# All big products of a hybrid attention block as seven block products instead of eight

## The chip, the core and the metric

The kernel runs on one core of a Trainium2 chip. Its time is the device time of one execution in microseconds, and the median of three runs is given. The engines work side by side, each with its own queue in order: TensorE (PE, with its loads of the stationary operand as PEld), VectorE (DVE), ScalarE (ACT), GpSimd (POOL), and SyncE (SP), whose queue issues nearly all transfers. A queue whose first instruction waits holds everything behind it.

## The reference

One layer over 512 tokens of width 2048 in float32:

```python
h = rms_norm(x, norm_gain)                       # 512 x 2048
proj = einsum('bsd,de->bse', h, w_in)            # 2048 -> 7184 columns
(sb_q, sb_k, sb_v, sb_g, gl_q, gl_k, gl_v, gl_g, gl_lr) = split(proj)
# group A: 8 heads x 128, q and k normed per head, stick-breaking attention
a_out = rms_norm(stick_breaking(q, k, v), sb_o_gain) * silu(sb_g)
# group B: 4 heads, gated linear attention; the decay comes from the 16 columns gl_lr
b_out = rms_norm(gla(gl_q, gl_k, gl_v, log_alpha), gla_o_gain) * silu(gl_g)
x = x + einsum('bse,ed->bsd', concat(a_out, b_out), w_out)   # 2048 -> 2048
```

The two einsums are the big products: 14 column groups of 512 in w_in (the 16 columns gl_lr apart) and 4 in w_out, each 512 tokens x 2048 x 512.

## The kernel before, in words

Every float32 operand of a big product is split into hi + lo, both of a format that TensorE takes in one pass (hi rounded by ScalarE, lo = value - hi by VectorE), and a product is the sum of three terms hi·hi, hi·lo, lo·hi. The 16 contraction tiles of h stay in SBUF as h_hi and h_lo for the whole kernel (lines 202 to 211); x is scaled by the norm's gain alone, and 1/rms of each token (rstd, rbc) is put in after the products.

`product` (line 173) makes one column group: four PSUM banks (128 tokens, or 128 columns, each), eight units of two contraction tiles. A unit's weights come from `weight_unit` (line 158): one 512 KB load by SP into a tile "st" (a ring of three), one cast on ScalarE, one subtraction on VectorE (tiles "hi" and "lo", rings of three), then 24 matmuls of 512 columns. Loads, splits and copies out of PSUM are under `urgent()`, which puts them ahead of other work of their engine.

Between the chunks of the products TensorE does the small work: the norm of x (`x_norm`, line 258: loads of x, squares on ScalarE, rstd, then four small matmuls that spread rstd along the free axis, bank rbc_ps), the gate ranks (`ranks`, `decays`), the attention heads and the GLA heads. These are chains of Python generators (class `Sides`): each step yields an amount of TensorE's work that shall lie before its next step, or a condition. TensorE's order is just the order in which the program is written out, so a step that finds its operands late stops TensorE; the other engines' orders are set by a scheduler when the kernel is built.

The order of the products (from line 632): q, k, v of the first four heads, the same of the other four, v, k, q and v of GLA, four groups of gates, four groups of the output. GpSimd makes constants and the masks of the attention (`affine_select`, lines 536 and 543).

Of the kernel before, what the change touches and what calls it, by code (L numbers as in the profile page):

```python
# [7 lines left out]
F32 = mybir.dt.float32  # L8
# [11 lines left out]
NU = NK // KU  # L20
NG_IN = 14           # 512-column groups of w_in (the 16 gate-rank columns apart)
# [10 lines left out]
NWK, NWT, NRING = 7, 6, 25      # tiles of the rings  # L32
URGENT = 1500                  # priority of what the tensor engine waits for
LAT_W = 14.0                   # tensor engine's work to put between a bank of scores and its weights
LAT_O = 12.0                   # the same, between an output and its normed value


class Sides:
# [42 lines left out]
def body(ctx: ExitStack, tc: tile.TileContext, x, xT, w_in, w_lr, w_alpha, vecs, w_out, out):  # L81
# [3 lines left out]
    hpool = ctx.enter_context(tc.tile_pool(name="hpool", bufs=1))  # L85
# [3 lines left out]
    ring = ctx.enter_context(tc.tile_pool(name="ring", bufs=1))  # L89
    pacc = ctx.enter_context(tc.tile_pool(name="pacc", bufs=4, space=PSUM))  # L90
# [32 lines left out]
    def room(n):  # L123
        return lambda: held[0] + n <= NRING

    def spl(name):
        return work.tile([P, S], F32R, name=name, tag="spl", bufs=8)
# [9 lines left out]
    def evac(dst, src, scale=None):  # L137
        """Copies that free a bank, by the two engines in turn."""
# [19 lines left out]
    def weight_unit(src, tag, beside=None):  # L158
        with urgent():
            st = wpool.tile([P, KU, S], F32, name=f"st_{tag}", tag="st", bufs=3)  # L160
# [12 lines left out]
    def product(src, a_hi, a_lo, tmajor, tag, before=None):
        """Four banks of a 512-column group; a_* hold the contraction on partitions."""
        acc = [pacc.tile([P, S], F32, name=f"acc_{tag}_{j}", tag="acc") for j in range(4)]
        for u in range(NU):
            beside = before(u) if before is not None else None
            hi, lo = weight_unit(src[u], f"{tag}_{u}", beside)
            for j in range(4):
                for i in range(KU):  # L180
                    k = u * KU + i
                    js = slice(j * P, (j + 1) * P)
                    first, last = k == 0, k == NK - 1
                    if tmajor:
                        terms = [(a_hi[k][:, js], hi[:, i, :]), (a_hi[k][:, js], lo[:, i, :]),
                                 (a_lo[k][:, js], hi[:, i, :])]
# [556 lines left out]
```

## Time and profile before

| | |
|---|---|
| median of 3 runs | 892.63 us (891.7 to 892.99) |
| span of the profiled execution, first to last instruction | 889.4 us |
| TensorE busy | 879.2 us, 99% |
| VectorE, ScalarE, GpSimd busy | 412.4, 364.7, 38.4 us |
| moved by DMA | 93.17 MB, mean 105 GB/s |

The span is the time inside the profiled execution; the timed runs also hold what lies around it. Busy is the time in which an engine had an instruction under way. Matmuls overlap, so their own durations (0.39 us) are longer than the distance from one start to the next; the distance is what counts. The granted clock of TensorE is 1.00 in every stretch.

### The profile page before, as it was taken

How to read it: one execution, taken by the hardware profiler on the slowest of the kernel's cores; microseconds unless marked ns; L12 is line 12 of the kernel's file. 1: busy time of each engine (PE TensorE's matmuls, PEld its weight loads, DVE VectorE, ACT ScalarE, POOL GpSimd, SP SyncE). 2: the span in 40 equal slices, each digit the busy share in tenths (PEclk: the TensorE clock that was granted, in tenths of full speed). 3: DMA queues.
4: the chain of work that ended last, by engine and by line, in shares of the span. 5: the costliest groups of instructions: out<-in, count | busy, mean ns of one | idle time of the engine just before them, and what ended most of it. 6: DMA issues, size and time to landing. Idle time of an engine off the chain costs nothing.

```text
span 889.4 us, 10463 instructions
## 1 busy us (share of the span) xinstructions
PE 879.2 (99%) x4090; PEld 728.9 (82%) x4090; DVE 412.4 (46%) x578; ACT 364.7 (41%) x712; POOL 38.4 (4%) x84
## 2 busy tenths in 40 slices
PE   8999999999999999999999999999999999999998
PEld 6888888888888887788888888888888888888886
DVE  6352343667545378655333444372727363232321
ACT  6762522467463276554112433372626362111110
POOL 1000000111000011210000000000000000000000
PEclk9999999999999999999999999999999999999999
DMA  9841222222222222122222221223232244443521
GB/s 340 283 142 50 95 94 95 71 80 87 72 71 94 76 72 72 67 71 86 95 102 73 71 77 66 74 93 99 100 104 100 95 143 147 137 165 120 177 83 48
DMA packets 30497, 93.17 MB, mean 105 GB/s; under 512 B 3536, under 2 KB 3664, under 8 KB 30448
## 3 DMA queue, kind: packets, MB, share of 16 engines
q1 hardware_dynamic: 28000, 88.29, 29.2%
q10 hardware_dynamic: 2448, 4.21, 1.3%
q8 instruction: 32, 0.52, 0.2%
q14 instruction: 17, 0.14, 0.0%
HBM read 88.30 MB, written 4.19 MB: 104 GB/s over the span
## 4 chain that ended last, share of the span: by engine, by line
PE 86%; issue 7%; DVE 3%; ACT 1%; POOL 1%; DMA 0%; SPq 0%; POOLq 0%; DVEq 0%; ACTq 0%
PE acc_g L99 20%; PE acc_o L99 20%; PE acc_k L99 10%; PE acc_q L99 10%; PE acc_sv L99 6%; PE acc_gv L99 5%; PE acc_gq L99 5%; PE acc_gk L99 4%; PE a L99 2%; PE o L99 1%; PE lr_ps L99 1%; PE kv L99 1%; DMA st_q<-in_w_in 0%; PE zB L99 0%; DVE cs_A L539 0%
## 5 line engine op out<-in xcount | busy, mean ns | idle before, releaser
L99 PE MATMUL acc_g<-h_hi,hi_g 128*128 128x512 f32 x256 | 101.4, 396 | 0.0
L99 PE MATMUL acc_g<-h_hi,lo_g 128*128 128x512 f32 x256 | 99.7, 390 | 0.0
L99 PE MATMUL acc_g<-h_lo,hi_g 128*128 128x512 f32 x256 | 99.6, 389 | 0.0
L99 PE MATMUL acc_o<-hi_o,mh 128*128 128x512 f32 x256 | 99.6, 389 | 0.0
L99 PE MATMUL acc_o<-lo_o,mh 128*128 128x512 f32 x256 | 99.6, 389 | 0.0
L99 PE MATMUL acc_o<-hi_o,ml 128*128 128x512 f32 x256 | 99.6, 389 | 0.0
L170 DVE TENSOR_TENSOR lo_o<-st_o,hi_o 128x1024 fp32r<-128x1024 f32 x32 | 39.2, 1224 | 110.1 <-ACT hi_o L169 101.7
L169 ACT CAST hi_o<-st_o 128x1024 fp32r<-128x1024 f32 x32 | 33.7, 1053 | 125.6 <-PE acc_o L99 116.8
L170 DVE TENSOR_TENSOR lo_g<-st_g,hi_g 128x1024 fp32r<-128x1024 f32 x32 | 39.2, 1223 | 74.4 <-ACT hi_g L169 74.4
L169 ACT CAST hi_g<-st_g 128x1024 fp32r<-128x1024 f32 x32 | 33.6, 1049 | 72.6 <-PE acc_g L99 65.9
L99 PEld LDWEIGHTS acc_g<-h_hi,lo_g 128*128 128x128 f32 x256 | 48.0, 188 | 10.2
L99 PEld LDWEIGHTS acc_o<-lo_o,mh 128*128 128x128 f32 x256 | 48.0, 188 | 10.1
L99 PEld LDWEIGHTS acc_o<-hi_o,mh 128*128 128x128 f32 x256 | 48.0, 188 | 10.0
L99 PEld LDWEIGHTS acc_g<-h_lo,hi_g 128*128 128x128 f32 x256 | 48.1, 188 | 9.8
L99 PEld LDWEIGHTS acc_o<-hi_o,ml 128*128 128x128 f32 x256 | 48.0, 188 | 9.8
L99 PEld LDWEIGHTS acc_g<-h_hi,hi_g 128*128 128x128 f32 x256 | 48.1, 188 | 9.6
L99 PE MATMUL acc_gv<-hi_gv,h_hi 128*128 128x512 f32 x128 | 52.1, 407 | 0.0
L99 PE MATMUL acc_k<-hi_k,h_hi 128*128 128x512 f32 x128 | 51.9, 405 | 0.0
L99 PE MATMUL acc_q<-hi_q,h_hi 128*128 128x512 f32 x128 | 50.5, 395 | 1.1 <-ACT hi_q L169 1.1
L99 PE MATMUL acc_sv<-hi_sv,h_hi 128*128 128x512 f32 x128 | 51.0, 398 | 0.0
L99 PE MATMUL acc_q<-lo_q,h_hi 128*128 128x512 f32 x128 | 50.0, 391 | 0.2 <-DVE lo_q L170 0.2
L99 PE MATMUL acc_k<-hi_k,h_lo 128*128 128x512 f32 x128 | 50.2, 392 | 0.0
(275 smaller groups left out, 1754.5 us busy)
## 6 DMA issues: line engine op xcount, KB each, us to landing
st_g<-in_w_in SPq DMA_DIRECT2D x32, 512.0 KB, 3.2
st_o<-in_w_out SPq DMA_DIRECT2D x32, 512.0 KB, 3.3
st_k<-in_w_in SPq DMA_DIRECT2D x16, 512.0 KB, 3.3
st_sv<-in_w_in SPq DMA_DIRECT2D x16, 512.0 KB, 3.2
st_gv<-in_w_in SPq DMA_DIRECT2D x16, 512.0 KB, 3.2
st_q<-in_w_in SPq DMA_DIRECT2D x15, 512.0 KB, 3.3
xk<-in_xT SPq DMA_DIRECT2D x16, 256.0 KB, 5.9
xt<-in_x SPq DMA_DIRECT2D x16, 256.0 KB, 5.2
```

What stands on the lines that cost most here:

```text
L99: nc.tensor.matmul(o, l, r, **kw)
L169: nc.scalar.copy(hi[:, p, :], st[:, p, :])
L170: nc.vector.tensor_tensor(lo[:, p, :], st[:, p, :], hi[:, p, :].bitcast(F32), ALU.subtract)
```

## The change

The tokens are cut in two halves of 256, the contraction in two halves (even and odd tiles), and the columns in two groups of 512. The eight products of such blocks become seven, with sums of blocks as operands (Strassen's scheme). `pair` does two column groups in four stages; in each stage it goes through four units of two contraction tiles (256 tokens x 256 of the contraction on the left, 256 of the contraction x 512 columns on the right):

- stage one: A11·B11 into the banks x, D·(B11 + B12) into y;
- stage two: NQ·(pw + B22) into x, S4·B22 into y;
- stage three: A12·B21 into y, S3·(pw - B11) into x; in the last unit these two are turned round;
- stage four: A22·(pw + B21) into x.

Here pw is a tile per unit ("pw", a ring of four) that holds the running sum of weight blocks. B11, B22, B21 and B11 once more are loaded into "st" (still a ring of three); in the order their names end in a, b, c and d and the unit's number. The sums of weights are made by VectorE but the last, pw + B21, by GpSimd. The sums of blocks of h (D, NQ, S4, S3) are made in the first pair by GpSimd and split there; D and S3 stay in SBUF, the other five split operands are written to DRAM ("far") and loaded again in every later pair, 512 KB per unit, into a ring of three tiles ("as"). Partial results leave the banks between the stages (stash) and are added at the end (finish). The pairs are (q0, k0), (q1, v0), (v1, k1), (GLA q, GLA k), (GLA v), two pairs of gates and two of the output. The third pair has the ranks' small matmuls between its block products, on its own left operands. In the pair "gqk" the weights are the stationary side and the 256 tokens the moving one, so its matmuls have 256 columns; in the others they keep 512. The output's left operand gets the same seven sums in its first pair. The gates and norms are rewritten for tiles of two halves, with the same arithmetic but for one activation less in the SiLU.

```diff
+    def load(src, tag, part="st"):
+            t = wpool.tile([P, KU, S], F32, name=f"{part}_{tag}", tag=part, bufs=HU if part == "pw" else 3)
+            nc.sync.dma_start(t, src)
+        return t
+
+    def split(t, tag):
+        with urgent():
+            nc.scalar.copy(hi, t)
+            nc.vector.tensor_tensor(lo, t, hi.bitcast(F32), ALU.subtract)
+    def add(o, a, b, op=ALU.add, eng=None):
+        with urgent():
+            (eng or nc.vector).tensor_tensor(o, a, b, op)
...
+                    t = work.tile([P, 2, KU, H2], F32R, name=name, tag="as", bufs=NAS)
+                    if key in self.far:
+                        nc.sync.dma_start(t.bitcast(F32), self.far[key])
+                        return t
...
+                if f not in self.keep:
+                    far = dram.tile([P, 2, KU, H2], F32, name=f"far_{name}")
+                    self.far[key] = far
+                    nc.sync.dma_start(far, t.bitcast(F32))
...
+        def mult(f, u, w, acc, start, stop):
+            t = A.get(f, u)
+            hi, lo = w
+            if tmajor:
+                for a in range(2):
+                    js = slice(a * P, (a + 1) * P)
+                    for i in range(KU):
+                        ah, al = t[:, 0, i, js], t[:, 1, i, js]
+                        for n, (l, r) in enumerate(((ah, hi[:, i]), (ah, lo[:, i]), (al, hi[:, i]))):
+                            mm(acc[a], l, r, start=start and i == 0 and n == 0,
+                               stop=stop and i == KU - 1 and n == 2, skip_group_check=True)
...
+        for u in order:
+            if before is not None:
+                before(0, u)
+            b11, pw[u] = load(s1[u], f"{tag}a{u}"), load(s2[u], f"{tag}{u}", "pw")
+            w = split(b11, f"{tag}a{u}")
+            mult("A11", u, w, x, u == first, u == last)
+            if before is not None:
+                before(1, u)
+            add(pw[u], pw[u], b11)
+            w = split(pw[u], f"{tag}p{u}")
+            mult("D", u, w, y, u == first, u == last)
+        m1 = o1.stash(x, 0, 1.0, f"{tag}m1")
+        m5 = o2.stash(y, 1, -1.0, f"{tag}m5")
+        for u in order:
+            if before is not None:
+                before(2, u)
+            b22 = load(s2[HU + u], f"{tag}b{u}")
+            add(pw[u], pw[u], b22)
+            w = split(pw[u], f"{tag}q{u}")
+            if u != last:
+                mult("NQ", u, w, x, False, False)
+                mult("S4", u, split(b22, f"{tag}b{u}"), y, False, False)
+            else:
+                v = split(b22, f"{tag}b{u}")
+                mult("S4", u, v, y, False, True)
+                y2 = o2.stash(y, 0, -1.0, f"{tag}y2")
+                mult("NQ", u, w, x, False, True)
+        o2.finish(x, 0, -1.0, y2)
+        for u in order:
+            if before is not None:
+                before(3, u)
+            b21, b11 = load(s1[HU + u], f"{tag}c{u}"), load(s1[u], f"{tag}d{u}")
+            w21 = split(b21, f"{tag}c{u}")
+            add(b11, pw[u], b11, ALU.subtract)
+            w3 = split(b11, f"{tag}d{u}")
+            add(pw[u], pw[u], b21, eng=nc.gpsimd)
+            if u != last:
+                mult("A12", u, w21, y, u == first, False)
+                mult("S3", u, w3, x, False, False)
+            else:
+                mult("S3", u, w3, x, False, True)
+                o2.finish(x, 1, -1.0, m5)
+                mult("A12", u, w21, y, False, True)
+        o1.finish(y, 0, 1.0, m1)
+        for u in order:
+            w = split(pw[u], f"{tag}e{u}")
+            mult("A22", u, w, x, False, u == last)
+        o1.finish(x, 1, 1.0, None)
...
+    pair(h, w_in[0], w_in[2], "qk", normed("q0", qn[0]), normed("k0", kn[0]), before=pair0)
+    side.spawn(x_norm())
+    side.until(lambda: "rstd" in done)
+    v[0] = ByToken("sv0", by_rstd)
+    pair(h, w_in[1], w_in[4], "qv", normed("q1", qn[1]), v[0])
+    side.spawn(attention(0, qn[0], kn[0], v[0]))
+    side.spawn(ranks())
...
+    pair(h, w_in[5], w_in[3], "vk", v[1], normed("k1", kn[1]), extra=rank_products)
+    pair(h, w_in[8], w_in[9], "gqk", qd, ki, tmajor=False)
+    pair(h, w_in[10], w_in[11], "gv", gv[0], gv[1])
+    pair(h, w_in[6], w_in[7], "ga", gate(0), gate(1))
+    pair(h, w_in[12], w_in[13], "gb", gate(2), gate(3))
...
+    pair(m, w_out[0], w_out[1], "o0", Residual(0), Residual(1), order=order, before=ready)
+    pair(m, w_out[2], w_out[3], "o1", Residual(2), Residual(3), order=order)
```

Two places where the order of the engines' instructions matters. First SP's queue in the middle of the second GLA value group: before, eight loads like these five, each waiting for the subtraction that frees its tile (the number at the end of a name is only the tile's).

```order
L166 DMA st_gv1_0_3949<-in_w_in 128x1024 [waits DMAHW2_49,DVE_49]
L166 DMA st_gv1_1_3985<-in_w_in 128x1024 [waits DMAHW3_49,DVE_49]
L166 DMA st_gv1_2_4042<-in_w_in 128x1024 [waits DMAHW4_49,DVE_49]
L166 DMA st_gv1_3_4119<-in_w_in 128x1024 [waits DMAHW5_49,DVE_49]
L166 DMA st_gv1_4_4157<-in_w_in 128x1024 [waits DMAHW6_49,DVE_49]
```

Now, the same weights in the pair "gv", from the end of stage two through stage three (far_ is the DRAM copy of a split left operand, h0 to h3 its units):

```order
L170 DMA st_gvd0_4612<-in_w_in 128x1024 [waits DMAHW7_49,DVE_49]
L245 DMA S4_h3_4575<-far_S4_h3_512 128x1024 [waits DMAHW3_49,PE_49]
L245 DMA NQ_h3_4593<-far_NQ_h3_533 128x1024 [waits DMAHW4_49,PE_49]
L170 DMA st_gvc1_4650<-in_w_in 128x1024 [waits DMAHW2_49,DVE_49]
L245 DMA A12_h0_4624<-far_A12_h0_583 128x1024 [waits DMAHW6_49,PE_49]
L170 DMA st_gvd1_4652<-in_w_in 128x1024 [waits DMAHW5_49,DVE_49,Pool_49]
L245 DMA A12_h1_4664<-far_A12_h1_631 128x1024 [waits DMAHW0_49,PE_49]
L170 DMA st_gvc2_4690<-in_w_in 128x1024 [waits DVE_49]
L245 DMA A12_h2_4704<-far_A12_h2_679 128x1024 [waits DMAHW7_49,DMAHW1_49,PE_49]
L170 DMA st_gvd2_4692<-in_w_in 128x1024 [waits DMAHW2_49,DVE_49,Pool_49]
L170 DMA st_gvc3_4730<-in_w_in 128x1024 [waits DVE_49]
...
L170 DMA st_gvd3_4732<-in_w_in 128x1024 [waits DMAHW6_49,DMAHW4_49,Pool_49]
```

Where a load waited for VectorE alone, the loads of d of units 1, 2 and 3 now also wait for GpSimd.

Second, TensorE's order around the small matmuls that spread rstd (rbc_ps). Before, they stood in the second group's product, after its fourth unit's first bank:

```order
L99 MATMUL acc_k0_0_601<-lo_k0_3_697,h_hi7_91 128x512
L99 MATMUL acc_k0_0_601<-hi_k0_3_696,h_lo7_107 128x512
L99 MATMUL rbc_ps_707<-dg0_484,runs_119 128x128 [waits Pool_49]
L99 MATMUL rbc_ps_707<-dg1_486,runs_119 128x128
L99 MATMUL acc_k0_1_602<-hi_k0_3_696,h_hi6_90 128x512
...
L99 MATMUL acc_k0_1_602<-hi_k0_3_696,h_lo7_107 128x512
L99 MATMUL rbc_ps_707<-dg2_710,runs_119 128x128 [waits DVE_49]
```

Now they stand in the second pair, between the last product of stage one (y) and the first of stage two (NQ of unit 0):

```order
L111 MATMUL y_qv1_948<-lo_qvp3_1118,D_h3_315 128x512
L111 MATMUL y_qv1_948<-hi_qvp3_1117,D_h3_315 128x512
L111 MATMUL rbc_ps_1133<-dg0_940,runs_86 128x128 [waits DVE_49,Pool_49]
L111 MATMUL rbc_ps_1133<-dg1_942,runs_86 128x128 [waits DVE_49]
L111 MATMUL x_qv0_945<-hi_qvq0_1151,NQ_h0_1155 128x512 [waits DMAHW4_49,Activation_49]
...
L111 MATMUL x_qv0_945<-hi_qvq0_1151,NQ_h0_1155 128x512
L111 MATMUL rbc_ps_1133<-dg2_1136,runs_86 128x128 [waits DVE_49]
L111 MATMUL rbc_ps_1133<-dg3_1138,runs_86 128x128 [waits DVE_49]
L111 MATMUL x_qv1_946<-hi_qvq0_1151,NQ_h0_1155 128x512 [waits Activation_49]
```

They moved from the middle of a stage to the seam of two stages, with the loads of x (eight of 512 KB) spread over that same pair's loads in SP's queue.

## Rows read from the trace of the kernel before

**Rows 1.** The page's first part: span, then busy us, share and count.

```profile
span 889.4 us, 10463 instructions
PE 879.2 (99%) x4090; PEld 728.9 (82%) x4090; DVE 412.4 (46%) x578; ACT 364.7 (41%) x712; POOL 38.4 (4%) x84
```

**Rows 2.** Stretches: start:end, length, busy by engine, granted clock, DMA share, GB/s.

```profile
0.00:22.00 22.00, 19.38 (x76) 13.66 (x77) 14.38 (x20) 14.45 (x19) 4.40 (x14) 1.00 0.92 339
...
616.00:660.00 44.00, 44.00 (x196) 36.44 (x195) 22.11 (x28) 20.05 (x30) 0.00 (x0) 1.00 0.28 96
```

**Rows 3.** Chain of waits, last pieces: start, length, what.

```profile
580.96 130.57 PE acc_g L99 x576
711.53 174.09 PE acc_o L99 x768
```

**Rows 4.** Timeline around six narrow matmuls: start, length, engine, line, what.

```profile
161.84 0.19 PEld L99 LDWEIGHTS zC<-hi_k,hi_q 128*128 128x128 f32 x1
162.06 0.28 PE L99 MATMUL zC<-hi_k,hi_q 128*128 128x256 f32 x1
...
162.78 0.40 PE L99 MATMUL acc_q<-hi_q,h_hi 128*128 128x512 f32 x1
```

**Rows 5.** Lines by form: count | busy us, mean ns | idle before.

```profile
L170 DVE TENSOR_TENSOR lo_g<-st_g,hi_g 128x1024 fp32r<-128x1024 f32 x32 | 39.2, 1223 | 74.4 <-ACT hi_g L169 74.4
L169 ACT CAST hi_g<-st_g 128x1024 fp32r<-128x1024 f32 x32 | 33.6, 1049 | 72.6 <-PE acc_g L99 65.9 <-PE acc_gv L99 6.6
...
L703 DVE TENSOR_TENSOR xr<-acc_o,xr 128x512 f32<-128x512 f32 x16 | 10.8, 688 | 15.6 <-PE acc_o L99 15.6
```

**Rows 6.** DMA issues: count, KB each, median us from issue to landing.

```profile
st_g<-in_w_in SPq DMA_DIRECT2D x32, 512.0 KB, 3.2
...
xk<-in_xT SPq DMA_DIRECT2D x16, 256.0 KB, 5.9
...
lr_st<-in_w_lr SPq DMA_DIRECT2D x1, 128.0 KB, 7.6
```

**Rows 7.** Lines of GpSimd alone, same columns as rows 5.

```profile
L543 POOL TENSOR_SCALAR_AFFINE_SELECT cs_A<-cs_A 128x128 f32<-128x128 f32 x8 | 5.6, 694 | 20.0 <-DVE cs_A L540 15.6 <-DVE v_q L487 2.2 <-PE acc_gk L99 2.2
...
L536 POOL TENSOR_SCALAR_AFFINE_SELECT e_A<-e_A 128x128 f32<-128x128 f32 x8 | 2.9, 356 | 38.7 <-DVE e_A L533 38.7
L430 POOL TENSOR_SCALAR_AFFINE_SELECT scT<-scT 128x512 f32<-128x512 f32 x4 | 2.7, 678 | 146.2 <-ACT scT L429 146.2
...
L220 POOL MEMSET runs<- 128x1024 f32 x1 | 1.0, 955 | 0.0
...
L216 POOL TENSOR_SCALAR_AFFINE_SELECT ident<-ident 128x128 f32<-128x128 f32 x1 | 0.3, 292 | 0.0
```

**Rows 8.** Timeline: a select of GpSimd beside a subtraction of VectorE.

```profile
353.22 1.22 DVE L170 TENSOR_TENSOR lo_gk<-st_gk,hi_gk 128x1024 fp32r<-128x1024 f32 x1
353.44 1.16 POOL L543 TENSOR_SCALAR_AFFINE_SELECT cs_A<-cs_A 128x128 f32<-128x128 f32 x1 [2.57 <-DVE cs_A L540]
```

**Rows 9.** Timeline of TensorE's start.

```profile
1.65 0.15 PEld L232 LDWEIGHTS <-warm 128*128 128x128 bf16 x1 [0.28 <-issue]
2.08 0.15 PEld L232 LDWEIGHTS <-warm 128*128 128x128 bf16 x1 [0.28 <-issue]
...
6.50 0.50 PE L99 MATMUL acc_q<-hi_q,h_hi 128*128 128x512 f32 x1 [1.15 <-ACT hi_q L169]
...
7.23 0.50 PE L99 MATMUL acc_q<-lo_q,h_hi 128*128 128x512 f32 x1 [0.22 <-DVE lo_q L170]
```

**Rows 10.** Timeline of the norm of x: last square and first diagonal tiles.

```profile
39.80 0.63 ACT L265 ACTIVATE xt<-xt 128x512 f32<-128x512 f32 x1
...
42.31 0.48 DVE L274 TENSOR_SCALAR dg<-ident,rstd 128x128 f32<-128x128 f32 x2
```

**Rows 11.** Timeline of SP's queue: the loads of x for the norm.

```profile
19.96 14.87 SPq L264 DMA_DIRECT2D xt<-in_x x14
```

More of the change, by code (lines that the diff above doesn't have):

```diff
@@ L20 @@
 NU = NK // KU
+HU = NU // 2
+H2 = 2 * P
 NG_IN = 14
@@ L35 @@
 LAT_O = 12.0
+ZMIN = -87.0
+FORMS = ("A11", "D", "NQ", "S4", "A12", "S3", "A22")
 class Sides:
@@ L69, in until @@
     def until(self, cond):
+        stuck = self.t + 2000.0
         while not cond():
+            assert self.t < stuck, "a chain waits for ever"
             t = self.t
@@ L123, in room @@
     def room(n):
-        return lambda: held[0] + n <= NRING
-    def spl(name):
-        return work.tile([P, S], F32R, name=name, tag="spl", bufs=8)
+        return lambda: held[0] + n <= NU4
     def sm(name, n):
@@ L171, in weight_unit @@
-        return hi, lo
[L173 to L186, printed above, removed]
-                    else:
-                        terms = [(hi[:, i, js], a_hi[k]), (hi[:, i, js], a_lo[k]),
-                                 (lo[:, i, js], a_hi[k])]
-                    for n, (l, r) in enumerate(terms):
-                        mm(acc[j], l, r, start=first and n == 0, stop=last and n == 2)
-                if u < NU - 1 or j == 3:
-                    side.step()
-        return acc
+            nc.scalar.copy(hi, t)
@@ L283, in x_norm @@
         done.add("rbc")
-    done = set()
     qe, ke, gm, low = [], [], [], []
+    lr = {}
     def ranks():
-        lr_st = wk("lr_st")
+        yield room(5)
+        st = ut("lr_st")
+        lr_st = st.rearrange("p a c -> p (a c)")
         nc.sync.dma_start(lr_st[:, 0:NK * RANK], w_lr)
+        HR = NK // 2 * RANK
+        w1, w2, wm, ws = (lr_st[:, i * HR:(i + 1) * HR] for i in range(4))
+        nc.vector.tensor_scalar(wm, w1, -1.0, None, ALU.mult)
+        nc.vector.tensor_tensor(ws, w1, w2, ALU.add)
+        for f, src in (("A11", w1), ("A12", w2), ("D", wm), ("A22", ws)):
+            t = ut(f"lr_{f}", F32R)
+            nc.gpsimd.memset(t.bitcast(F32), 0.0)
+            t8 = t.rearrange("p a (k c) -> p (a k) c", c=P)
+            s8 = src.rearrange("p (k r) -> p k r", r=RANK)
+            nc.scalar.copy(t8[:, :, 0:RANK], s8)
+            nc.vector.tensor_tensor(t8[:, :, RANK:2 * RANK], s8, t8[:, :, 0:RANK].bitcast(F32), ALU.subtract)
+            lr[f] = t8
+        drop(1)
+        yield room(1)
         wst = wk("wa_st")
@@ L324, in ranks, with rank_products @@
-        nc.gpsimd.memset(lrT.bitcast(F32), 0.0)
-        nc.scalar.copy(lrT[0:32, :], lst[0:32, :])
-        nc.scalar.copy(lrT[64:96, :], lst[0:32, :])
-        nc.vector.tensor_tensor(lrT[32:64, :], lst[0:32, :], lrT[0:32, :].bitcast(F32), ALU.subtract)
-        low.extend([wa, lrT])
-    def decays():
-        yield room(1)
-        wa, lrT = low
-        blk = rt("blk")
+        low.append(wl)
+        done.add("ranks")
+    def rank_products(f, u, t):
+        if f not in ("A11", "A12", "D", "A22"):
+            return
+        side.until(lambda: "ranks" in done)
+        if "ps" not in lr:
+            lr["ps"] = ptile("lr_ps")
+            lr["n"] = 0
+        ts = slice(0, H2) if f in ("A11", "A12") else slice(H2, S)
+        for i in range(KU):
+            for hl in range(2):
+                lr["n"] += 1
+                mm(lr["ps"][:, ts], lr[f][:, u * KU + i, :], t[:, hl, i], start=lr["n"] == 1, stop=lr["n"] == 4 * NK,
+                   skip_group_check=True)
+        if lr["n"] == 4 * NK:
+            drop(4)
+            side.until(lambda: "rbc" in done)
+            ps, wl = lr["ps"], low[0]
+            lst = wk("lr_f")
+            nc.vector.tensor_tensor(lst[0:32, :], ps[0:32, :], rbc[0:32, :], ALU.mult)
+            lrT = wl[:, 1, :]
+            nc.scalar.copy(lrT[0:32, :], lst[0:32, :])
+            nc.scalar.copy(lrT[64:96, :], lst[0:32, :])
+            nc.vector.tensor_tensor(lrT[32:64, :], lst[0:32, :], lrT[0:32, :].bitcast(F32), ALU.subtract)
+            done.add("lr")
```

570 lines of the change are left out of this document (343 added, 227 removed).

## Prediction

> **What bounds the kernel now.** I read the page's first two parts, then the chain of waits, the costliest lines, the stretches, and last the other queues. TensorE is busy 99% of the span [rows 1], and in the gate stretch every microsecond, while VectorE works 22.1 of 44 us, ScalarE 20 and the DMA engines 28% [rows 2]. The chain's longest pieces are TensorE's own products: 576 gate matmuls in 130.57 us and 768 output matmuls in 174.09 us [rows 3], 0.2267 us each, nothing between them. So time falls only if TensorE gets less work, and only as far as VectorE, GpSimd and the queues still deliver in time.
>
> **What the change removes.** 18 column groups x 4 banks x 16 contraction tiles x 3 terms are 3456 matmuls, x 0.2267 = 783.4 us. Now a pair of groups takes 7 block products x 4 units x 12 = 336 instead of 384. Eight pairs keep 512 columns: 2688 x 0.2267 = 609.3. The pair "gqk" (w_in 8 and 9) has 672 matmuls of 256 columns; six such stand in a row from 162.06 to 162.78 [rows 4], 0.12 us each, so 80.6 us, though each load of the stationary side lasts 0.19 [rows 4] (128 us is the upper end, were those loads not to overlap; the six show that they do). Saved: 783.4 - 689.9 = 93.5 us. The rest of TensorE's work stays, within 1 us.
>
> **What it adds beside TensorE.** 28 splits per pair instead of 16: a cast of 1.05 us and a subtraction of 1.22 [rows 5], and 12 sums of 1.22 on VectorE and 4 on GpSimd. VectorE so has 40 x 1.22 = 49 us, with the bank copies (7 x 0.69, as xr's [rows 5]) 54 us, of a pair's 76.2. On the mean that is hidden. Loads are 40 x 524 KB = 21 MB per pair; 96 GB/s took 0.28 of the DMA engines [rows 2], so 343 GB/s would fill them, and 21 MB take 61 of 76 us: hidden too, if they start early enough. Where they don't is the sum.
>
> **Stage three of each pair.** Weight loads rotate over three tiles "st". The load of unit u+1's b11 ("d" in the order) takes the tile of unit u's b21 ("c"), which GpSimd frees by its sum pw + b21; that sum may overwrite pw only after VectorE's pw - b11, which waits for the load of d of unit u. So one step is load, subtraction, GpSimd sum, and again. Zero is the end of S4 of unit 2; a block product is 12 x 0.2267 = 2.72 us. TensorE wants S3 of unit 2 at 7 x 2.72 = 19.0, and S3 of unit 3 at 21.8, for the last unit turns its two products round. Unit 0's d gets a split tile when NQ of unit 3 ends, 5.44; cast and subtraction to 7.8, a bank copy to 8.5, then VectorE makes d of unit 1, done 9.7. Now GpSimd's sum. The trace has no two-input operation of it. The nearest rows: a 128x1024 memset took 0.96 us, a 128x512 select 0.68, a 128x128 one 0.29 [rows 7]; so one input of 1024 costs some 1.2 us (0.16 + 1024 x 1.0 ns), two inputs 1.2 to 2.4; I take 1.8, the middle, for the rows are as near to the one as to the other. But GpSimd is held while VectorE reads two inputs from SBUF: a select of 0.29 us took 1.16 when it met lo_gk, and ended 0.16 us after it [rows 8]. VectorE has three splits to make from 9.7 to 13.8, with 0.5 us between; I credit 0.3 more at its changes. The sum ends at 14.8. The load of d takes 3.3 (3.2 [rows 6] and the issue before it), 18.1; subtraction 19.4; cast and lo 21.7: S3 of unit 2 starts at 21.5 (its second matmul is the first to read lo), 2.4 late. GpSimd again: 1.05 free during the cast, held by two subtractions (2.45), 0.75: 23.6. Load 26.9, subtraction 28.2, cast and lo 30.5: S3 of unit 3 starts at 30.3 where 24.2 was due, 6.1 late. Together 8.5 us per pair. The same steps with unheld sums of 1.2 us give 1.6; held ones of 2.4 give 9.7; and with loads of 5.9, as xk's [rows 6], 14.9. Six pairs have little else in this stage; in the two with attention TensorE's small work stretches each unit, and I count half. 6 x 8.5 + 2 x 4 = 59 us (10 to 119).
>
> [...]
>
> **Stage four.** The load of A22 of unit 2 stands in SP's queue behind two weight loads that wait for the split of unit 1, which itself waits for the last product of stage three: 2.4 + 0.35 + 3.3 = 6.05 us where two products cover 5.44. 0.7 x 9 = 6 us (0 to 12).
>
> **The norm of x.** It now runs beside the second pair. In the order its last five loads stand behind the load of S4's left operand and wait for the split of b22, 22 us into the pair; 6 x 524 KB at 343 GB/s land 9 us later. From the last square (start 39.80) to the diagonal tile (42.31) it took 2.5 us before [rows 10]; now the square is 1.05 instead of 0.63, and in TensorE's order the sums "rbc" stand ahead of NQ. TensorE ends stage one at 21.8, and goes on at about 34.9: 13 us (8 to 16). The cover that it had, loads issued from 19.96 to 34.83 [rows 11] beside a running product, is gone.
>
> **The gate ranks** in the third pair: their weights load late in SP's queue (lr_st took 7.6 us in the crowd of the start [rows 6]; I take 4) and TensorE has four matmuls on them after the first block product. Load, two small sums, cast, subtraction end at about 9.5; TensorE is there at 4.5, and waits some more for the second set: 6 us (0 to 8).
>
> **The first pair** also makes its seven left operands. Before, the first product began at 6.50, and had lo at 7.23 [rows 9]. Now ScalarE's queue casts a0 and p0 first: a0 lands at 5.5, cast 6.6, lo 7.8, sum 9.0, cast of p0 10.1, cast of A11 10.7, lo 12.0: 5 us later. Stage one: each write to DRAM waits in SP's queue for a split, and the next x load behind it: 3 us. Stage two: VectorE has 3 x 1.22 + 2 x 0.69 = 5.0 of each 5.44 us: 4. Stage three, GpSimd held nearly always: 12. Stage four 1. Sum 25 us (15 to 40). The first output pair does the same without x: 6 us more than others (2 to 10).
>
> **Sum.** -93.5 + 59 + 6 + 13 + 6 + 25 + 6 = +21.5 on the profiled execution, whose span is 889.4 [rows 1]; the median of the timed runs, 892.63, is 3.2 us above it. Forecast 914 us.
>
> **Rivals.**
> 1. Faster: the GpSimd sums are short and not held, stage three costs 1.6 per pair. 21.5 - 59 + 13 = -24.5: 868 us. The side turns at (59 - 21.5) / 7 = 5.4 us per pair. For it: the selects e_A took 0.36 on the mean, near the 0.29 of an unheld one. Against: cs_A, issued while VectorE was busy, took 0.69 [rows 7], and VectorE will have less idle time.
> 2. All of it is hidden but the start: 892.6 - 93.5 + 5 = 804 us. Against it stand the waits in the orders above.
> [...]
> 4. DMA is full: stages one to three ask 1.57 MB per 5.44 us, 289 GB/s of 343. If loads last 5.9 as xk's did at 339 GB/s [rows 2, 6], 8 x 5.2 = 42 us more: 956.
> 5. Narrow matmuls run at 0.19 [rows 4]: +47, 961.
>
> **Chances.** Forecast 0.33; rivals 0.28, 0.04, 0.21, 0.11, 0.03. A difference under 0.2% can't be told from none. Faster 0.32, same 0.05, slower 0.63. Range 858 to 955; the likeliest case alone is 895 to 932.
>
> **What would show it.** Right: TensorE's matmuls sum to some 95 us less and its idle time is over 100 us, most of it before S3 and ended by splits of d; SP waits for GpSimd's pw; GpSimd's sums mean over 2.5 us, shortest near 1.7; VectorE near 690 us; a gap of over 10 us before rbc near 130 us; first product at 11. Wrong, if GpSimd's sums end within 1.5 us, if d's loads wait for nothing of GpSimd, or if the gap before rbc is under 3 us.

## The result and the profile after

The changed kernel takes 1009.88 us (median of 4 runs, 1006.98 to 1011.29) against 892.73 us: 1.1316 times as long (95% interval 1.1295 to 1.1337). The forecast was 914, its range 858 to 955: the sign was right, the size far off.

The page's first part and the granted clock in 40 slices, after:

```profile
span 1005.3 us, 11406 instructions
...
PE 854.1 (85%) x4034; PEld 704.8 (70%) x4034; DVE 749.3 (75%) x808; ACT 494.1 (49%) x839; POOL 221.7 (22%) x163
...
PEclk7989996988998989898899999998898898989998
```

Against [rows 1], TensorE is busy 85% instead of 99%, and VectorE 749 us instead of 412. The clock, 1.00 throughout before [rows 2], now falls in many parts of the span (9 is 0.9 or more): its records show 24 stretches at half, 156 us together.

To split the 115.9 us between the spans I took the distance from each matmul's start to the next one's, against the usual distance of its shape in the kernel before (0.227 us for 512 columns; 0.120 for 256 columns of the products). What goes beyond it, up to 2.15 times, is counted as slowed, beyond that as waiting (in a half-clock stretch, beyond twice):

| us | before | after | difference |
|---|---|---|---|
| work at the usual distance | 867.8 | 777.7 | -90.1 |
| slowed | 9.7 | 59.9 | +50.2 |
| waiting | 6.5 | 162.4 | +155.9 |

Of the 59.9, 48.1 lie in half-clock stretches. So the saving is there, and what took it back twice over is waits and the clock. The stretches of the nine pairs (start:end, length, busy us by engine with counts, granted clock, DMA share, GB/s), in the order qk, qv, vk, gqk, gv, ga, gb, o0, o1:

```profile
10.90:125.20 114.30, 91.32 (x336) 69.53 (x336) 91.42 (x78) 61.47 (x125) 56.90 (x30) 0.88 0.66 226
125.20:229.70 104.50, 83.34 (x344) 67.45 (x345) 66.96 (x76) 48.72 (x88) 15.63 (x9) 0.89 0.71 247
229.70:368.70 139.00, 120.61 (x619) 101.59 (x619) 109.33 (x149) 84.26 (x193) 27.77 (x38) 0.93 0.48 166
368.70:502.10 133.40, 114.26 (x861) 111.33 (x859) 109.79 (x143) 79.26 (x153) 26.76 (x36) 0.91 0.43 149
502.10:585.20 83.10, 79.00 (x336) 64.01 (x337) 57.90 (x47) 33.43 (x35) 11.28 (x4) 0.98 0.70 248
585.20:700.20 115.00, 105.52 (x478) 86.03 (x477) 86.04 (x107) 54.72 (x95) 15.78 (x8) 0.97 0.58 198
700.20:803.00 102.80, 87.23 (x370) 71.23 (x369) 75.18 (x70) 51.78 (x60) 15.50 (x6) 0.90 0.58 205
803.00:913.40 110.40, 88.54 (x353) 68.54 (x352) 91.67 (x88) 48.06 (x63) 34.83 (x18) 0.92 0.61 212
913.40:1005.30 91.90, 80.43 (x337) 63.83 (x335) 57.69 (x52) 27.27 (x26) 11.18 (x4) 0.96 0.65 226
```

Only gv, with no small work beside it, comes near its 76.2 us. The output, 174.1 us in the chain of before [rows 3], now takes 110.4 + 91.9. What TensorE waited for, largest first (total, times, longest):

```profile
PE mT L115 <- DVE ge L917: 24.4, 7, 5.4
PE rbc_ps L111 <- DVE dg L546: 15.4, 1, 15.4
PE x_qk L111 <- ACT A_h L253: 12.0, 3, 5.8
PE x_o L111 <- DVE lo_o0d L178: 5.5, 3, 2.0
PE T_q L115 <- DVE gm L654: 5.4, 1, 5.4
PE x_qk L111 <- DVE lo_qkd L178: 4.7, 3, 1.9
PE lr_ps L111 <- DVE r_q L764: 4.5, 1, 4.5
PE T_k L115 <- DVE lr_f L614: 3.9, 1, 3.9
```

The largest, mT, is no product at all: it is the gates' turning matmuls. Counted by starts, the waits are 50.2 us before products of a split of d, 25.6 before mT, 27.9 before other small work of attention, decays and GLA, 15.7 before rbc. The other 43 lie before the ranks' products (4.7) and before products of the other splits, 23 of them in the first pair.

One step of stage three in the pair gv, all engines, shows the chain that the prediction described and what it got wrong in it (timeline: start, length, engine, line, what, idle before and who ended it):

```profile
562.54 1.23 DVE L183 TENSOR_TENSOR st_gvd<-pw_gv,st_gvd 128x1024 f32<-128x1024 f32 x1 [1.04 <-DMA st_gvd<-in_w_in]
...
563.88 1.04 ACT L177 CAST hi_gvd<-st_gvd 128x1024 fp32r<-128x1024 f32 x1 [4.94 <-DVE st_gvd L183]
563.90 2.35 POOL L183 TENSOR_TENSOR pw_gv<-pw_gv,st_gvc 128x1024 f32<-128x1024 f32 x1 [4.62 <-DVE st_gvd L183]
...
564.96 2.38 DVE L178 TENSOR_TENSOR lo_gvd<-st_gvd,hi_gvd 128x1024 fp32r<-128x1024 f32 x1 [1.19 <-ACT hi_gvd L177]
...
564.98 0.50 PE L111 MATMUL x_gv<-hi_gvd,S_h 128*128 128x512 f32 x1 [1.77 <-ACT hi_gvd L177]
...
567.40 0.68 PE L111 MATMUL x_gv<-lo_gvd,S_h 128*128 128x512 f32 x1 [1.91 <-DVE lo_gvd L178]
```

TensorE's own rows just after (x2 is two matmuls in one row):

```profile
568.73 0.63 PE L111 MATMUL x_gv<-lo_gvd,S_h 128*128 128x512 f32 x1
569.16 1.05 PE L111 MATMUL x_gv<-hi_gvd,S_h 128*128 128x512 f32 x2
570.01 0.63 PE L111 MATMUL x_gv<-lo_gvd,S_h 128*128 128x512 f32 x1
```

In the first, the load of d lands, VectorE subtracts, and ScalarE's cast and GpSimd's sum start together. The sum takes 2.35 us, and it was VectorE's lo that was held: 2.38 us instead of 1.22 [rows 5], until 1.1 us after the sum's end. TensorE waited 1.77 and 1.91 us, and then its matmuls stand 0.43 apart (568.73, 569.16, a pair, 570.01). The clock fell right behind these two waits, neither of them 2 us long; the stretch there:

```profile
567.90:570.90 3.00, 3.00 (x9) 2.32 (x8) 1.33 (x2) 0.00 (x0) 0.00 (x0) 0.50 0.92 309
```

Granted clock 0.50. Where VectorE's two-input work met a sum of GpSimd in gv, at least one of them took longer: this lo_gvd 2.38 us instead of 1.22, and two of GpSimd's four sums (539.70 and 548.85) 3.26, where the one at 773.09 in gb, which met no two-input work of VectorE, took 2.37.

### The profile page after: what moved, and what is told of

Same layout as the page of the kernel before. It is cut to its first block, busy times and chain, and to the rows that moved or that the text cites. A ratio compares the mean times of both kernels' runs of the same rounds, so it can differ in the third digit from the quotient of the medians.

```text
span 1005.3 us, 11406 instructions
## 1 busy us (share of the span) xinstructions
PE 854.1 (85%) x4034; PEld 704.8 (70%) x4034; DVE 749.3 (75%) x808; ACT 494.1 (49%) x839; POOL 221.7 (22%) x163
## 5 line engine op out<-in xcount | busy, mean ns | idle before, releaser
L183 POOL TENSOR_TENSOR pw_qv<-pw_qv,st_qvc 128x1024 f32<-128x1024 f32 x4 | 11.2, 2796 | 93.0 <-DVE st_qvd L183 93.0
L183 POOL TENSOR_TENSOR pw_gb<-pw_gb,st_gbc 128x1024 f32<-128x1024 f32 x4 | 12.0, 3004 | 86.7 <-DVE st_gbd L183 81.9
L183 POOL TENSOR_TENSOR pw_gv<-pw_gv,st_gvc 128x1024 f32<-128x1024 f32 x4 | 11.3, 2819 | 81.2 <-DVE st_gvd L183 81.2
L183 POOL TENSOR_TENSOR pw_o<-pw_o,st_o1c 128x1024 f32<-128x1024 f32 x4 | 11.2, 2794 | 77.8 <-DVE st_o1d L183 77.8
L111 PE MATMUL x_qk<-hi_qka,A_h 128*128 128x512 f32 x32 | 14.0, 506 | 12.9 <-ACT A_h L253 12.0
L111 PEld LDWEIGHTS x_qk<-hi_qka,A_h 128*128 128x128 f32 x32 | 7.4, 240 | 17.1 <-ACT A_h L253 13.4
L183 POOL TENSOR_TENSOR pw_ga<-pw_ga,st_gac 128x1024 f32<-128x1024 f32 x4 | 11.3, 2837 | 34.4 <-DVE st_gad L183 21.9
L111 PE MATMUL y_o<-hi_o0p,D_m 128*128 128x512 f32 x32 | 13.8, 498 | 5.0 <-ACT D_m L253 2.5
L111 PE MATMUL x_gqk<-S_h,hi_gqkd 128*128 128x256 f32 x64 | 15.2, 338 | 3.2 <-ACT hi_gqkd L177 3.2
L183 POOL TENSOR_TENSOR pw_qk<-pw_qk,st_qkc 128x1024 f32<-128x1024 f32 x4 | 10.9, 2718 | 22.2 <-DVE st_qkd L183 22.2
L183 POOL TENSOR_TENSOR pw_vk<-pw_vk,st_vkc 128x1024 f32<-128x1024 f32 x4 | 10.4, 2607 | 23.5 <-DVE st_vkd L183 10.5
L111 PE MATMUL x_vk<-hi_vkd,S_h 128*128 128x512 f32 x32 | 12.6, 440 | 3.2 <-DVE n_k L374 3.2
L111 PEld LDWEIGHTS x_gqk<-S_h,hi_gqkd 128*128 128x128 f32 x64 | 12.7, 243 | 3.4 <-ACT hi_gqkd L177 3.4
```

Of the source, the lines that this page charges most:

```text
L183: (eng or nc.vector).tensor_tensor(o, a, b, op)
```

## The experiments

Two theories stood at the start. A: each group of waits has its own local cause, as the orders of the queues show it, and the clock adds to every wait. B: VectorE, DMA or latency is the bound, so that mending one wait moves it. The kernels build on the changed one. Waits, "half" (time at the lower clock) and VectorE's busy time are of the profiled execution; times are medians, ratios to the kernel before on the same chip with their 95% intervals.

| run | us | ratio | waits | half | VectorE |
|---|---|---|---|---|---|
| the changed kernel | 1009.9 | 1.1295 to 1.1337 | 162 | 156 | 749 |
| e1_ring4 | 983.5 | 1.0977 to 1.1069 | 143 | 133 | 756 |
| e2_sum_dve | 970.4 | 1.0864 to 1.0899 | 133 | 132 | 742 |
| e3_norm_early | 1002.6 | 1.1196 to 1.1285 | 155 | 160 | 749 |
| e4_fill | 1004.4 | 1.1238 to 1.1289 | 140 | 114 | 749 |
| e5_dve_ring4 | 954.3 | 1.0655 to 1.0730 | 128 | 107 | 737 |
| e6_no_pool_sums | 937.4 | 1.0467 to 1.0561 | 111 | 96 | 734 |
| e7_far_act | 947.7 | 1.0591 to 1.0648 | 125 | 90 | 734 |
| e8_gates | 918.9 | 1.0259 to 1.0327 | 98 | 86 | 734 |
| e9_pool_queue | 909.2 | 1.0172 to 1.0230 | 85 | 61 | 733 |
| e10_urgent | 895.6 | 1.0004 to 1.0050 | 80 | 46 | 732 |
| e11_reload_pool | 904.6 | 1.0115 to 1.0167 | 87 | 36 | 732 |
| e12_old_output | 906.1 | 1.0124 to 1.0156 | 70 | 40 | 645 |
| e13_spread | 898.5 | 1.0065 to 1.0095 | 79 | 49 | 732 |
| e14_no_sums | 865.3 | 0.9680 to 0.9715 | 51 | 47 | 575 |
| e15_norm_pool | 998.5 | 1.1130 to 1.1220 | 152 | 139 | 748 |
| e16_dma_sums | 914.9 | 1.0227 to 1.0287 | 97 | 71 | 688 |

### Stage three: e1, e2, e5

```diff
-tag=part, bufs=HU if part == "pw" else 3)      # e1: NU4 also 26 -> 25
+tag=part, bufs=HU)
-add(pw[u], pw[u], b21, eng=nc.gpsimd)          # e2; e5 has both edits
+add(pw[u], pw[u], b21)
```

> The tiles of the weight loads (st) are four instead of three; to make room the ring of long-lived tiles has 25 instead of 26, which moves some of the attention's small matmuls in the pair gqk. With four tiles the load of d of a unit no longer needs the tile that the GpSimd sum frees. Theory A (the chain load of d, pw - b11, GpSimd sum, next load is what makes TensorE wait in stage three): the waits before products of the splits of d, 50 us in all now, fall under 10, the half-clock stretches that follow them go too (some 15 us), time 945 to 960. Theory B (VectorE's backlog or the speed of the loads makes d late): the waits before d stay over 30 us, time over 985. The GpSimd sums keep their length in both.

> The sum pw + b21 is made by VectorE instead of GpSimd, 36 sums of 1.22 us instead of 2.4 to 3.3. Theory A (the length of the chain's GpSimd link sets the waits of stage three): the link is 1.2 to 2.5 us shorter per unit, the waits before d fall from 50 to about 20 us, time 965 to 980. Theory B (VectorE, 749 us busy, is what the rest waits for): its 44 us more make the attention's and the gates' small work later, the waits before it grow from some 50 to over 70, time 1000 to 1030.

> Both edits of the first two runs: the sum pw + b21 by VectorE, and four tiles st (25 long-lived tiles). Theory A (two ways to break one chain, and the waits before d that the VectorE sum left, some 20 us, go with the fourth tile): 945 to 958, waits before d under 5 us. Theory B (what is left of them is VectorE's backlog): 962 to 975, waits before d over 15 us.

The waits before d fell from 50.2 to 18.1, 16.8 and, with both, 5.6 us: the chain was the cause, and either way of breaking it takes two thirds. e1 missed theory A's figures, under 10 us of these waits and 945 to 960: it left the GpSimd sums, 36 of 2.35 us and more, beside VectorE's, and e5, which differs from e1 in the engine of these sums alone, is 29 us faster. e2 is the telling one. The page's line of e2:

```profile
PE 845.4 (87%) x4034; PEld 703.1 (72%) x4034; DVE 741.8 (76%) x844; ACT 496.6 (51%) x839; POOL 130.2 (13%) x127
```

VectorE has 36 instructions more, 44 us at 1.22, and is busy 7.5 us less than in the changed kernel. So those sums on GpSimd had cost VectorE some 52 us of its own (an estimate from these two runs).

### GpSimd beside VectorE: e6

```diff
-tt = nc.gpsimd.tensor_tensor         # also in _q; likewise the scaling in load_x
+tt = nc.vector.tensor_tensor
```

> As e5_dve_ring4, and the sums of the left operands and the scaling by the norm's gain, which GpSimd makes in the first pair and the first output pair, go to VectorE too. Theory A (GpSimd's two-input and scaling work of the start is slow, 1.3 to 2.5 us for 128x512, and while it runs VectorE's own instructions take 1.8 to 3 us instead of 1.22, so that moving it costs VectorE nothing): VectorE's busy time rises by less than 15 us though it gets some 35 us of work, waits in the first pair fall by 10 to 15, in the first output pair by 3 to 6: 15 to 22 us under e5_dve_ring4. Theory B (each engine's time is its own): VectorE's busy time rises by 30 to 40 us and the first pair is no faster: within 5 us of e5_dve_ring4, or slower.

17 us under e5. VectorE took 44 instructions more and is busy 3 us less. Lines by form of VectorE's lo in the first pair of e5 (count | busy us, mean ns | idle before):

```profile
L178 DVE TENSOR_TENSOR lo_qkp<-pw_qk,hi_qkp 128x1024 fp32r<-128x1024 f32 x4 | 6.8, 1702 | 2.5 <-ACT hi_qkp L177 2.5
...
L178 DVE TENSOR_TENSOR lo_qkb<-st_qkb,hi_qkb 128x1024 fp32r<-128x1024 f32 x4 | 6.5, 1613 | 4.2 <-ACT hi_qkb L177 4.2
```

The same lines in e6:

```profile
L178 DVE TENSOR_TENSOR lo_qkp<-pw_qk,hi_qkp 128x1024 fp32r<-128x1024 f32 x4 | 4.9, 1225 | 1.8 <-ACT hi_qkp L177 1.8
...
L178 DVE TENSOR_TENSOR lo_qkb<-st_qkb,hi_qkb 128x1024 fp32r<-128x1024 f32 x4 | 4.9, 1222 | 0.0
```

The same instructions, 1702 and 1225 ns, 1613 and 1222. (That of d, 2268 ns in the changed kernel, was back at 1221 in e5, where the sum pw + b21 had gone from GpSimd.) The first pair's waits fell from 23.9 (e5) to 12.8 us: A.

### The gates and the small work: e8, e10, e13

In the changed kernel the last gate's turn shows how small work came late. VectorE, timeline (TensorE's last product had begun at 792.93, and mT followed at 798.68):

```profile
787.47 1.22 DVE L914 TENSOR_TENSOR ge<-ge,z 128x1024 f32<-128x1024 f32 x1
788.61 1.22 DVE L178 TENSOR_TENSOR lo_gbe<-pw_gb,hi_gbe 128x1024 fp32r<-128x1024 f32 x1
...
796.18 1.23 DVE L183 TENSOR_TENSOR pw_o<-pw_o,st_o0a 128x1024 f32<-128x1024 f32 x1 [0.60 <-DMA st_o0a<-in_w_out]
797.32 1.22 DVE L917 TENSOR_TENSOR ge<-ge,on 128x1024 f32<-128x1024 f32 x1
```

Between two multiplications of one gate lie eight splits and sums that have precedence, all but the first of the next pair; before the last of them VectorE itself stood 0.60 us for a load, with the gate's second multiplication behind it.

```diff
 # e8, on e6: the gate's ScalarE and VectorE steps
+with urgent():
-    yield 8.0
+    yield 16.0
 # e10, on e9: turned(), weights(), the copies of mT and the ranks' sums
+with urgent():
 # e13, on e10: rbc 60 us after the norm; decays 9 us apart instead of 3
```

> As e6_no_pool_sums, and the vector work of the gates stands ahead of other work of its engines like the weights' splits, with 16 us of TensorE's work between it and the gates' turning matmuls (mT) instead of 8. Theory A (the waits before mT, 26 to 30 us so far, are the gates' chain of two ScalarE-VectorE rounds standing behind splits and sums on a VectorE that is busy three quarters of the time): waits before mT under 10 us, half-clock stretches after them go: 18 to 28 us under e6_no_pool_sums. Theory B (the splits that are pushed back cost the same elsewhere): within 8 us of it.

> As e9_pool_queue, and the steps by which ScalarE and VectorE free a PSUM bank of the small work (the turned q and k, the difference of the scores, the copies of the turned weights and of the gates) and the ranks' few sums stand ahead of other work like the splits. Theory A (TensorE waits there for its PSUM banks and operands behind splits on a VectorE that is busy 80%): the waits before T_q, T_k, wT, lg and mT, 42 us in e8_gates, fall by half or more, with the clock 15 to 30 us under e9_pool_queue. Theory B (VectorE is full in these stretches, and what goes first makes the splits late): within 6 us of e9_pool_queue, waits before products instead.

> As e10_urgent, with 60 us of TensorE's work between the norm of x and the matmuls that spread rstd instead of 22, and 9 us instead of 3 between the four decays, whose ScalarE and VectorE work stands beside the turned q and k in the pair gqk. Theory A (these are local crowds: 3.5 us before rbc and some 7 before T_q and T_k in gqk go): 880 to 890. Theory B (the crowd only comes later, before the pair's second sums, which need the decays): within 4 us of e10_urgent's 895.6.

e8: waits before mT from 33.7 to 10.4 us, time 18.5 us under e6: A. Precedence and the longer distance were changed together; no run parts them. e10: mT to 0, 13.6 us under e9 with half-clock time from 61 to 46, just under A's range; the waits of the other small work fell only from 29.9 to 23.0, and waits before d rose from 8.8 to 14.7, so part of it moved, as B said. e13: rbc's wait went, the waits of the small work rose from 23.0 to 31.0, and the time stayed within 3 us: B. The crowd only came later:

```profile
PE T_k L115 <- DVE cs_A L810: 13.1, 2, 9.7
PE wT_B L115 <- ACT cs_B L815: 8.0, 2, 5.4
```

### The norm of x and the queues: e3, e15, e9, e7, e11

In the changed kernel SP issued x's loads among those that wait, and the last four 2.2 us after TensorE's last product had begun (SP's queue; then TensorE):

```profile
134.57 0.90 SPq L533 DMA_DIRECT2D xt<-in_x  x2
...
144.60 0.33 SPq L245 DMA_DIRECT2D NQ_h<-far_NQ_h  x1
144.98 0.42 SPq L533 DMA_DIRECT2D xt<-in_x  x1
148.73 0.33 SPq L170 DMA_DIRECT2D st_qvb<-in_w_in  x1
149.11 1.95 SPq L533 DMA_DIRECT2D xt<-in_x  x4
```

```profile
146.90 0.39 PE L111 MATMUL y_qv<-hi_qvp,D_h 128*128 128x512 f32 x1
162.68 0.55 PE L111 MATMUL rbc_ps<-dg,runs 128*128 128x128 f32 x1 [15.39 <-DVE dg L546]
```

Before, such loads ran beside a product [rows 10, 11].

```diff
 # e3: x_norm starts in the first pair's last unit of stage three, urgent; rbc 60 us later
 # e15: one edit
-nc.sync.dma_start(xt.rearrange(
+nc.gpsimd.dma_start(xt.rearrange(
 # e9, on e8: so too the writes of "far" and w_lr; ranks() before the second pair
 # e7, on e6: the writes of "far" by nc.scalar
 # e11, on e10: reloads from the pair gv on by nc.gpsimd; rbc 60 us later
```

> The loads of x for the norm start in the last unit of the first pair's stage three instead of beside the second pair, ahead of its weights in SP's queue, and the four matmuls that spread rstd stand 60 us of TensorE's work later instead of 22. Theory A (the wait of 15.6 us before them is the loads standing behind others in SP's queue): the wait goes, and of the half-clock stretch after it (17 us, 8.5 lost) most: 980 to 990. Theory B (the wait only moves: the copy of y out of PSUM at the end of stage one needs rstd too, or the 4 MB crowd out the second pair's first weights): under 8 us gained, 1002 or more.

> The changed kernel with one edit: the eight loads of x for the norm are issued by GpSimd's queue instead of SP's; nothing else moves. Theory A (the wait of 15.7 us before rbc is the loads standing behind others in SP's queue): the wait falls under 4 us and the half-clock stretch after it (17 us, 8.5 lost) goes: 985 to 992. Theory B (the loads and the squares themselves take that long, or they crowd out the pair's weights): the wait stays over 8 us or others of that size come in the same pair: 998 to 1010.

> As e8_gates, and GpSimd's queue, nearly empty by now, issues the writes of the split left operands to DRAM, the loads of x for the norm and the load of the ranks' weights; the ranks' weights are prepared beside the second pair instead of the third. Theory A (what was late there stood behind other waits in SP's queue; on a queue that nothing else needs, the wait costs nobody): the waits before rbc (15.7 us) and before the ranks' products (6.0) fall under 4 together, the first pair's before the left operands (8.5) fall by some 4, and the half-clock stretches after them go: 885 to 897. Theory B (the 4 MB themselves need the time, or transfers issued by GpSimd are slower): rbc keeps over 8 us: 905 to 920.

> As e6_no_pool_sums, and the writes of the split left operands to DRAM are issued from ScalarE's queue instead of SP's. Theory A (in SP's queue each such write waits for VectorE's split and holds the loads behind it; waits on them are 94 us of SP's time): 5 to 12 us under e6_no_pool_sums, nearly all in the first pair. Theory B (the writes then hold ScalarE's casts instead, or the loads weren't late for that): within 3 us of it or slower.

> As e10_urgent, and from the pair gv on GpSimd's queue issues the reloads of the left operands (each waits for TensorE to free its tile, some 100 us of SP's time in all), and the matmuls that spread rstd stand 60 us of TensorE's work after the norm of x instead of 22. Theory A (in SP's queue these waits hold the weights' loads behind them): the waits ended by SP's reloads, some 11 us, and that before rbc, 3.5, go: 882 to 890. Theory B (the reloads are late for their tiles, not for the queue, or GpSimd's issue costs as much): within 4 us of e10_urgent.

e15: the wait before rbc went entirely and the pair qv has 14.3 us less of waits, as A said; but the time is only 11.4 us shorter, at the edge of B. The other pairs wait 4.3 us longer, and time at the lower clock fell by 18 us but what is lost there not at all (48.1 and 49.8). The stretch of 17.1 us that A priced at 8.5 lay in the wait itself for the most part, so its matmuls had lost only 2.4 us. In the changed kernel (busy by engine, TensorE first, then the granted clock):

```profile
151.10:162.60 11.50, 0.00 (x0) 0.00 (x0) 2.71 (x11) 6.02 (x13) 0.00 (x0) 0.50 0.57 196
162.60:168.20 5.60, 5.52 (x17) 4.77 (x18) 4.87 (x17) 1.73 (x6) 0.00 (x0) 0.50 0.02 3
```

e3 cut the wait before rbc to 1.8 us but gained 7.2 us: its 4 MB stood ahead of the second pair's weights (pw_qv landed after 6.9 us instead of 4.3), and 5.7 us of waits came there: mostly B. e9: rbc's wait to 2.9, the ranks' to 0; but the same pair now waits 5.4 us for its own weights and left operands, and the time is 9.7 us under e8, in B's range, not A's 22 or more. e7 and e11 lost 10.3 and 9.0 us: e7 as B had it, e11 beyond what either theory allowed. In e7 the waits rose most in the output pairs (16.2 to 26.9); that the writes held ScalarE's casts there is likely, not shown. In e11 reloads issued by GpSimd landed after 5.1 us (4.3 on SP's queue), and the waits in gv rose from 0.5 to 5.6. In these runs x's loads on a queue that nothing else needed no longer waited; reloads on it, or writes on ScalarE's queue, cost time.

### The clock: e4

```diff
+for n in range(14):
+    nc.tensor.matmul(x[0], zero[:, 0:P], zero, start=False, stop=False, skip_group_check=True)
 mult("S3", u, w3, x, False, True)
```

> Before the product with S3 of the last unit of stage three, in every pair, 14 matmuls of zeros (512 columns, 3.2 us at the upper clock) are added to the bank x, so that TensorE works where it stood still; no wait and no transfer is changed. Theory A (each stop of some 4 us lets the granted clock fall, and the products after it take 0.427 us instead of 0.227): the stretches at the lower clock after these places, 51 us in eight of nine pairs, mostly vanish, worth up to 25 us; where a pair has no wait there the zeros cost up to 3.2 us: 988 to 1000. Theory B (the clock falls for another reason, or the lost time is the wait itself): no gain, and what isn't hidden is added: 1010 to 1025.

The mean clock rose from 0.923 to 0.944, time at half from 156 to 114 us, and what products lost there from 48.1 to 37.2. At these places seven pairs of the changed kernel had 44 us at the lower clock; with the zeros 3.4 us are left, in one pair. The pair o1 from the start of its S3 of the last unit, in the changed kernel and then in e4 (the clock is 0.50, then 1.00):

```profile
980.90:987.40 6.50, 4.79 (x10) 3.42 (x11) 4.20 (x3) 0.98 (x2) 1.36 (x1) 0.50 0.00 0
```

```profile
979.20:985.00 5.80, 4.81 (x21) 3.63 (x20) 4.25 (x5) 1.17 (x2) 0.51 (x1) 1.00 0.13 45
```

Theory A's mechanism: the fall follows the standing still, since work on zeros in its place prevents it. TensorE's work rose by 25.5 us (the zeros), waits fell by 22.4 and the slowed part by 7.4. So the zeros cost 3 us more than they spared in waits, and the net gain (4.4 us between the spans, 5.5 between the medians) is what is left of the clock's 7.4. The time, 1004.4, lies between A's range and B's: 42 us less at the lower clock were worth 10.9 us in the products, not half of 42, since part of such a stretch is waiting itself. Behind the zeros the granted clock is 1.00 in eight of the nine pairs.

### What is left: e14, e12, e16

```diff
 # e14, on e10: left out
-add(pw[u], pw[u], b11)   # and b22, pw - b11, b21
 # e12, on e11: the four output groups by eight block products, as before
 # e16, on e10 (rbc as e13), pairs gv to o1; the same for b21
-add(pw[u], pw[u], b22)
+nc.gpsimd.dma_start(pw[u], s2[HU + u], accum_op=ALU.add)
```

> As e10_urgent, but the four sums of weight blocks per unit are left out (144 instructions of 1.22 us on VectorE; each product takes the block itself, so the result is another). All loads, splits and products stay. Theory A (what is left of the waits, 80 us, is VectorE's load, 732 us of 895): VectorE falls to some 560 us, the waits to under 45, the loss at the lower clock with them: 835 to 860. Theory B (they are latencies: a load, a cast, a subtraction and a turn, whatever VectorE's load): waits over 65, 880 or more.

> As e11_reload_pool, but the four output groups go by eight block products as before the change, with a whole hi and lo of the gated output and no left sums; the nine pairs become seven. Theory A (a pair that also makes its left operands asks more of VectorE than its shorter time has: in e10_urgent the two output pairs lose 21 us in waits and 8 at the lower clock, against 21.8 us of TensorE's work saved): TensorE's work rises by 21.8 us, nearly all of the 29 go, and VectorE's busy time falls by 80 to 100 us: 4 to 9 us under e11_reload_pool. Theory B (the saving is worth its price there): 5 to 20 us over e11_reload_pool.

> As e13_spread without its spaced decays (that is e10_urgent with the later rbc), and in the five pairs from gv on the sums pw + b22 and pw + b21 are made by the DMA engines: GpSimd's queue issues a second load of the block that adds into pw, long before pw is split. 40 instructions of 1.22 us leave VectorE (49 us), 21 MB more move. Theory A (as e14_no_sums says, VectorE's load is a third of what is left, and these sums aren't needed soon): VectorE falls to some 685 us, waits in the output pairs from 21 to under 14: 878 to 888. Theory B (the adding transfers are slow or crowd the other loads, 290 to 340 GB/s already in places): waits for loads come instead: 893 to 910.

e14 is 30.3 us under e10, with VectorE at 575 us and waits at 51, a little over A's range in time and waits: a third of the waits that were left hung on these sums. Whether by VectorE's load or because a sum is also a link between a load and its split, the run does not part: waits before d fell from 14.7 to 1.2, where the sum was such a link, and those of the small work from 23.0 to 13.2, where it was not. What the remaining 51 hang on is open. e12: VectorE fell by 87 us and the waits by 17, TensorE's work rose by 21.4, and the time is the same as e11's (906.1 and 904.6): neither theory; in the output the scheme is worth just what it costs. e16: VectorE fell to 688 us as A said, but the time rose by 19 us over e10, past B's range too. The adding loads landed late (median us to landing: the changed kernel's plain loads of b22, then e16's plain and adding ones):

```profile
st_gvb<-in_w_in SPq DMA_DIRECT2D x4, 512.0 KB, 3.8
```

```profile
st_gvb<-in_w_in SPq DMA_DIRECT2D x4, 512.0 KB, 6.5
...
pw_gv<-in_w_in POOLq DMA_DIRECT2D x8, 512.0 KB, 7.7
```

The plain loads beside them became slower too, so the adding, GpSimd's queue and the crowd of transfers are not parted here.

No version that computes the whole beat the kernel before: e10 comes to 1.0027 of it. It has the mends that helped, and VectorE is busy 82% of its span:

```profile
PE 822.9 (92%) x4034; PEld 679.6 (76%) x4034; DVE 732.1 (82%) x888; ACT 494.6 (55%) x839; POOL 76.3 (9%) x132
```

## Why the prediction was wrong

**What held.** The saving, 93.5 us forecast, 90.1 measured. The chain of stage three, by e1, e2 and e5. The norm: 13 forecast, 15.7. Ranks: 6 and 4.8. The first pair: 25 (15 to 40) and 31.4, with the first product at 10.94 for 11; its parts came out less well (start and stage one 14.3 us for 8, stage two 8.7 for 4, stage three 8.5 for 12), so that the sum is near is partly luck. The sign was not: the waits that the sum names came to some 103 us, and these alone outweigh the saving. The first output pair: 6 forecast beyond the others, and 8.6 before its products of D and of b22. VectorE 690 forecast, 749; e2 and e6 say why: GpSimd held it.

**Mis-sized.** Stage four, 6 us, measured 0.8. Stage three, 59 us in eight pairs, measured 41.7 counted by starts (50.2 with the first pair's 8.5). GpSimd's sum was taken as 1.8 us alone; it takes some 2.37. But held by VectorE it was taken as 5.1 us (9.7 to 14.8) and then 4.2 (19.4 to 23.6), and in gv those two sums took 3.26 and 2.41: 3.6 us of the 3.9 by which gv's 4.6 us of waits stayed under the 8.5 of the sum. And the step looked at one side only: GpSimd held by VectorE [rows 8], not VectorE by GpSimd.

**The two steps that failed.** First, "On the mean that is hidden": VectorE's load was set against a pair's length, and only the products' chains were followed. For TensorE's other work the sum has no term at all ("The rest of TensorE's work stays, within 1 us"). The small work, with several steps of ScalarE and VectorE between two turns on TensorE, stood behind the added splits and sums, which have precedence: 25.6 + 27.9 us before it, 4.7 before the change. e8 and e10 took mT's away by changing precedence and distance alone. A mean load of 75% did not tell what the work last in line would wait.

Second, the clock. The sum has no term for it. A clock that falls was the third of the rivals, at 0.21: the author's estimate, which no row of the kernel before shows, where the granted clock is 1.00 [rows 2]. Measured, 23 stretches with products lost 48.1 us at the lower clock, 2.1 each, up to 2.9, and in gv the clock fell behind two waits under 2 us. The sum held 115 us of waits already, and e4 shows that the fall follows the standing still: 44 us at the lower clock at its places, 3.4 with work on zeros there.

Sum of the miss, 1005.3 - 910.9 (the forecast span) = 94.4 us: 50.2 by the clock and other slowing, 155.9 - 115 = 40.9 in waits (53.5 - 4.7 = 48.8 of small work not named, less 8 over-estimated in the rest), 3.4 of saving.

What stays open: whether the 23.0 us of the small work's waits in e10 could be had by another placing of its steps (e13 only moved them).

## What to carry to other kernels

Fewer matmuls help a kernel at 99% TensorE only if every other engine's work, with its precedence, still meets its due time; follow the work that comes last in line, not the mean load. Where TensorE stands still, add the loss at the lower clock: here 0.3 us on the mean for each microsecond waited (48.1 us beside 162.4). And sums are not free on the idle engine: 36 sums on GpSimd took from VectorE some 52 us, where VectorE needed 44 for them.

## What was not expected of the hardware

- Moving 36 sums from GpSimd to VectorE made VectorE's busy time shorter (749.3 to 741.8 us).
- Right behind two waits of 1.77 and 1.91 us, with 0.5 us of work between them, the granted clock was 0.50.
- In e16 loads that add into SBUF landed after 7.6 to 8.0 us by pair, plain loads of the pair gv beside them after 4.1 to 6.5, and after 3.2 to 4.4 in the changed kernel.
